# One shared set of four PSUM banks for the small matmuls of a hybrid decoder trunk, with small matmuls of one array tiling put together, the last-needed operand first, and the cumulative sum on the whole TensorE array

## The chip, the cores and the metric

The kernel runs on one core of one Trainium2 chip. The metric is the device time in microseconds (us) of one execution. The work is done by five engines that run side by side and wait for each other through semaphores: PE (TensorE, matrix multiplication), DVE (VectorE), ACT (ScalarE), POOL (GpSimd) and SP (SyncE, which issues most of the DMA transfers). Matmul results land in PSUM, which has eight banks of 128 partitions by 2 KB.

## The reference

Two layers on 256 tokens of width 1024. Each layer has three token mixers that are fed by one input projection, and then a feed-forward block.

```python
for l in range(DEPTH):                       # DEPTH = 2
    h = _rmsnorm(x, mix_norm[l])
    proj = (h @ w_in[l]).astype(jnp.float32)
    ret_c, fox_c, rwkv_c, gate_c = jnp.split(proj, splits, axis=-1)
    y_ret = _retention_branch(ret_c, ret_gn[l])          # q k^T * decay, then v; per head norm
    y_fox = _fox_branch(fox_c, ...)                      # softmax attention with a cumulated log forget gate
    y_rwkv = _rwkv7_branch(rwkv_c, ...)                  # recurrent state of 64x64 per head
    gates = jax.nn.sigmoid(gate_c).reshape(B, S, N_BRANCH, D)
    merged = (gates[:, :, 0] * (y_ret @ p_ret[l]) + gates[:, :, 1] * (y_fox @ p_fox[l])
              + gates[:, :, 2] * (y_rwkv @ p_rwkv[l]))
    x = x + merged @ w_out[l]
    h = _rmsnorm(x, ffn_norm[l])
    g, u = jnp.split(h @ w_gate_up[l], 2, axis=-1)
    x = x + (jax.nn.silu(g) * u) @ w_down[l]             # D_FF = 2816
```

Every mixer has four heads of 64 channels. All data are float32.

## The kernel before, in words

Large products. A float32 product is made of three matmuls with rounded operands (`mm3`, L304, L307, L308): high part by high part, low part of the data by high part of the weights, high by low. The weights come from HBM in pieces of 1 MB (tile `raw`, three buffers, issued by SP in the order in which they are used). ACT makes the high half `whi` of each (L287) and DVE the low half `wlo` (L288), 128x1024 at a time, four buffers each. On PE these products are rows named `mm`, `mv` and `mqk`, with 256 moving columns on the whole 128x128 array.

Small products. The mixers need many matmuls with 64 or 32 rows or columns. These run in a part of the array: the rows of the trace write the tiling as 64*128, 128*64, 64*64 or 32*32 (rows*columns of one part). Two heads of a pair lie in partitions 0 to 63 and 64 to 127, so their matmuls can use different parts.

- `rwkv`: the recurrence is cut into four chunks of 64 tokens (`NC` = 4, `C` = 64), 16 units for 2 head pairs `a`, 4 chunks `q` and 2 heads `h`. `pgm` (L807) are the masked products within a chunk, which DVE writes to `gg`; `ptr` (L842) are transposes. A triangular system is solved in steps: SP stores 16x16 blocks (`d`, L819), loads them rearranged (`lt`, L822), a loop on DVE inverts them (`ti`), SP stores (`d`, L872) and loads them again (`tb`, L877), DVE transposes (`dn`, L882, one instruction for each head `h`), and PE combines the blocks to 32 and 64 (`pn1` L887, `pn2` L894, `px1` L906, `px2` L914). Then `pu`, `par` (L935), `pU` (L947), the state from chunk to chunk `pS` (L957), and the output `py` (L972 within the chunk, L980 from the state).
- `fox`: the cumulative sum of the gates `pc` (L1061, L1062), scores `pl` (L1099) with the causal mask added by a matmul (L1101), transposes `px`, output `pyf` (L1123 to L1125).
- `ret`: scores `psc` (L1183, L1184), times the decay mask on DVE (`rsc`, L1185, L1186), output `pyr` (L1191 to L1193), head norm with `pnr` and `pvr`.

PSUM. Its eight banks are in three sets: four for the large products (tag `mm`), two for `rwkv` (tag `rw`), two for `fox`, `ret` and the norms (tag `fr`). A tile waits until the tile that had its bank before has been read.

What sets the order. `rwkv`, `fox`, `ret` and `gemms` (gate projections and merges) are generators. `mixers` takes turns among them: each `yield` gives a due time from the table `PACE`, and the generator that is due first goes on. The order of instructions on each engine comes from this program order and a scheduler that estimates when operands are ready. On the chip each engine works through its own list in that order. After the mixers a layer has the output projection, 22 pairs of gate and up columns, and the down projection, which are large products only.

Of the kernel before, what the change touches and what calls it, by code (L numbers as in the profile page):

```python
# [31 lines left out]
AHEAD = 3  # L32
PACE = {'hp_piece': 4.0, 'hp_gemm': 0.0, 'hp_rwkv': 0.0, 'hp_fox': 0.0, 'hp_ret': 0.0, 'hp_merge': 44.0, 'hp_turn': 0.0, 'gemms0': 3.04, 'gemms1': 3.31, 'gemms2': 5.65, 'gemms3': 3.34, 'gemms4': 32.96, 'gemms5': 10.98, 'rwkv0': 10.21, 'rwkv1': 11.2, 'rwkv2': 8.93, 'rwkv3': 1.29, 'rwkv4': 4.68, 'rwkv5': 0.99, 'rwkv6': 10.9, 'rwkv7': 6.78, 'rwkv8': 3.67, 'rwkv9': 15.39, 'rwkv10': 0.0, 'rwkv11': 0.1, 'rwkv12': 0.0, 'rwkv13': 4.53, 'rwkv14': 10.11, 'rwkv15': 3.46, 'rwkv16': 46.63, 'rwkv17': 6.78, 'rwkv18': 7.88, 'rwkv19': 1.76, 'fox0': 6.98, 'fox2': 4.26, 'fox3': 4.47, 'fox4': 9.38, 'ret0': 2.57, 'ret1': 2.4, 'ret2': 16.22, 'rwkv24': 0.61, 'rwkv22': 8.91, 'rwkv23': 25.79, 'rwkv20': 4.99, 'fox5': 10.77, 'ret4': 6.18, 'ret3': 0.0}
# [123 lines left out]
class Kernel:  # L157
    def __init__(self, ctx, tc, d, depth=DEPTH, debug=None):
# [15 lines left out]
        pz = self.ps.tile([P, T], F32, tag="fr", bufs=2, name="pz")  # L174
# [282 lines left out]
    def rstd(self):  # L457
# [6 lines left out]
        pn = self.ps.tile([P, 2], F32, tag="fr", bufs=2, name=self.nm("pn"))  # L464
# [24 lines left out]
    def gemm_n(self, width, xs, name="mv"):  # L489
        ps = [self.ps.tile([P, width], F32, tag="mm", name=self.nm(name)) for _ in range(2)]  # L490
# [48 lines left out]
    def mixers(self, l, xs):  # L539
# [87 lines left out]
    def ffn(self, l):  # L627
# [3 lines left out]
        with ExitStack() as st:  # L631
# [4 lines left out]
            for j in range(FT // 2):  # L636
                if j == 0:
                    pg = self.gemm_halves(xs, 7, tag="rw")
# [63 lines left out]
    def rwkv(self, l, rw):  # L702
# [3 lines left out]
        pt = lambda n: self.ps.tile([P, 2, T], F32, tag="rw", bufs=2, name=self.nm(n))  # L706
# [45 lines left out]
        pn = self.ps.tile([P, 2, 4], F32, tag="rw", bufs=2, name=self.nm("pnk"))  # L752
# [48 lines left out]
        for a in range(2):  # L801
            pg2 = [self.ps.tile([P, NC, 2 * C], F32, tag="rw", bufs=2, name=self.nm("pgm")) for _ in range(2)]
# [52 lines left out]
        pm = self.ps.tile([P, NP, 64], F32, tag="rw", bufs=2, name=self.nm("pm"))  # L855
# [35 lines left out]
        px = self.ps.tile([P, NP, C], F32, tag="rw", bufs=2, name=self.nm("pn2"))  # L891
# [29 lines left out]
        for a in range(2):  # L921
            pu = self.ps.tile([P, NC, 2 * C], F32, tag="rw", bufs=2, name=self.nm("pu"))
# [7 lines left out]
        for a in range(2):  # L930
            pa = self.ps.tile([P, NC - 1, 2 * C], F32, tag="rw", bufs=2, name=self.nm("par"))
# [10 lines left out]
        pu = self.ps.tile([P, 2, NC - 1, 64], F32, tag="rw", bufs=2, name=self.nm("pU"))  # L942
        for q in range(NC - 1):
            for a in range(2):
                for h in range(2):
                    u = unit(a, q, h)
                    nc.tensor.matmul(pu[hs[h], a, q, :], gg[:, u, 0:C], uw[:, u, :], start=q == a == 0, stop=q == NC - 2 and a == 1,  # L947
                                     tile_position=(0, h * 64))
        us = self.t2.tile([P, 2, NC - 1, 64], F32, tag="t2", name=self.nm("us"))
# [16 lines left out]
        py = [self.ps.tile([P, 2, 2, C], F32, tag="rw", bufs=2, name=self.nm("py")) for _ in range(2)]  # L966
        for q2 in range(NC // 2):
            for a in range(2):
                for h in range(2):
                    for e in range(2):  # L970
                        u = unit(a, 2 * q2 + e, h)
                        nc.tensor.matmul(py[h][hs[e], q2, a, :], gg[:, u, C:2 * C], uw[:, u, :], start=q2 == a == 0, stop=False,  # L972
                                         tile_position=(0, e * 64))
# [64 lines left out]
    def fox(self, l, fx):  # L1038
# [22 lines left out]
        nc.tensor.matmul(pc[0:8, :], lf[:, 0, :], c["tri"][:, 0, :], start=True, stop=False)  # L1061
        nc.tensor.matmul(pc[0:8, P:T], lf[:, 1, :], c["tri"][:, 1, P:T], start=False, stop=True)  # L1062
# [25 lines left out]
        for t in range(2):  # L1088
# [31 lines left out]
        for h in range(4):  # L1120
            a, s = h // 2, slice((h % 2) * 64, (h % 2) * 64 + 64)
            vs = slice(h * 64, h * 64 + 64)
            nc.tensor.matmul(py[s, a, 0:P], v[:, 0, vs], pT0[:, h, 0:P], start=True, stop=True)  # L1123
            nc.tensor.matmul(py[s, a, P:T], v[:, 0, vs], pT0[:, h, P:T], start=True, stop=False)
            nc.tensor.matmul(py[s, a, P:T], v[:, 1, vs], pT1[:, h, :], start=False, stop=True)  # L1125
# [116 lines left out]
```

## Time and profile before

| | |
|---|---|
| median of three runs | 795.45 us (795.17 to 798.04) |
| the profiled execution: its own time, its span | 795.98 us, 794.0 us |
| busy: PE, PEld (weight loads), DVE, ACT, POOL | 785.9, 761.8, 569.4, 403.6, 15.0 us |
| matmuls | 7010 |
| read from HBM, written | 136.97 MB, 1.33 MB |
| granted TensorE clock | 1.000 |

The span is the time from the first to the last instruction. Rows of the timeline give the start, the duration, the engine, the line of the kernel, the operation, the tile written and the tiles read, the tiling of the array (for PE) and the size; "x8" stands for eight instructions drawn as one row, and a bracket tells how long the engine had stood idle before the row and who released it. A float32 matmul of a small product shows as two records on PE (128 moving columns of `pgm`, one instruction, are two). Matmuls overlap on PE, so the distance between starts, not the duration, says what one costs. Layer 0's mixers lie at about 40 to 170 us, layer 1's at about 430 to 560 us.

### The profile page before, as it was taken

The page shows a single profiled execution, that of the slowest core. Times are in us where ns is not written, and L with a number is a line of the kernel's source. Part 1 is how long each engine was busy: PE and PEld are TensorE (multiplying, and loading weights), DVE is VectorE, ACT ScalarE, POOL GpSimd, SP SyncE. Part 2 cuts the span into 40 slices and gives each one's busy share as a digit, 9 for nine tenths or more (in the row PEclk, how much of TensorE's full clock was granted, in tenths as well). Part 3 has the DMA queues.
Part 4 walks back from the last instruction along what each step waited for, and adds up shares of the span by engine and source line. Part 5 has one row for each costly group of instructions (what it writes and reads, how often), then busy time and mean ns, then how long its engine had stood idle before and what let it go on. Part 6 is the DMA issues. An engine that isn't in the chain of part 4 may idle for free.

```text
span 794.0 us, 16539 instructions
## 1 busy us (share of the span) xinstructions
PE 785.9 (99%) x7010; PEld 761.8 (96%) x7010; DVE 569.4 (72%) x919; ACT 403.6 (51%) x563; POOL 15.0 (2%) x51
## 2 busy tenths in 40 slices
PE   8999999999999999999999999999999999999998
PEld 7999999999999999999998998998999999999998
DVE  5887888778866666656668798877787766666453
ACT  6577445345646544535446773544356544444331
POOL 3000000000000000000020000000000000000000
PEclk9999999999999999999999999999999999999999
DMA  8755434425555555555564453442355465564650
GB/s 319 259 173 181 152 118 167 133 74 220 192 193 201 178 206 193 171 195 199 199 203 174 174 173 111 167 166 81 134 213 211 161 213 176 196 210 162 208 192 27
DMA packets 28234, 140.42 MB, mean 177 GB/s; under 512 B 7648, under 2 KB 9216, under 8 KB 13184
## 3 DMA queue, kind: packets, MB, share of 16 engines
q1 hardware_dynamic: 28016, 139.10, 50.5%
q8 instruction: 55, 0.90, 0.5%
q10 hardware_dynamic: 144, 0.26, 0.1%
q14 instruction: 19, 0.16, 0.1%
HBM read 136.97 MB, written 1.33 MB: 174 GB/s over the span
## 4 chain that ended last, share of the span: by engine, by line
PE 94%; DVE 2%; DMA 2%; ACT 1%; issue 0%; SPq 0%; DVEq 0%; ACTq 0%
PE mm L304 27%; PE mm L307 27%; PE mm L308 27%; DVE wlo L288 1%; PE mqk L487 1%; PE mqk L486 1%; PE mqk L485 1%; DMA raw<-in_win 1%; ACT whi L287 1%; PE mv L485 1%; PE pgm L807 1%; PE mv L486 1%; PE mv L487 1%; DMA rsw<-rqk 1%; PE ptr L842 1%; PE psc L1183 0%
## 5 line engine op out<-in xcount | busy, mean ns | idle before, releaser
L287 ACT CAST whi<-raw 128x1024 fp32r<-128x1024 f32 (+1 forms) x257 | 264.9, 1033 | 311.4 <-PE mm L307 220.6
L288 DVE TENSOR_TENSOR wlo<-raw,whi 128x1024 fp32r<-128x1024 f32 (+1 forms) x257 | 308.7, 1203 | 152.0 <-ACT whi L287 151.4
L304 PE MATMUL mm<-xh,whi 128*128 128x256 f32 x1312 | 367.6, 280 | 1.6 <-ACT whi L287 1.3
L308 PE MATMUL mm<-xh,wlo 128*128 128x256 f32 x1264 | 351.0, 278 | 0.1
L307 PE MATMUL mm<-xl,whi 128*128 128x256 f32 x1264 | 350.6, 277 | 0.1
L304 PEld LDWEIGHTS mm<-xh,whi 128*128 128x128 f32 x1312 | 246.6, 188 | 4.0 <-ACT whi L287 1.5
L307 PEld LDWEIGHTS mm<-xl,whi 128*128 128x128 f32 x1264 | 237.5, 188 | 1.4 <-issue 0.5
L308 PEld LDWEIGHTS mm<-xh,wlo 128*128 128x128 f32 x1264 | 237.3, 188 | 1.1 <-issue 0.3
L307 PE MATMUL mm<-lo,whi 128*128 128x256 f32 x576 | 160.2, 278 | 0.2
L308 PE MATMUL mm<-hi,wlo 128*128 128x256 f32 x576 | 160.2, 278 | 0.0
L304 PE MATMUL mm<-hi,whi 128*128 128x256 f32 x576 | 160.0, 278 | 0.0
L307 PEld LDWEIGHTS mm<-lo,whi 128*128 128x128 f32 x576 | 108.2, 188 | 1.0 <-DVE lo L425 0.6
L304 PEld LDWEIGHTS mm<-hi,whi 128*128 128x128 f32 x576 | 108.2, 188 | 0.6 <-issue 0.3
L308 PEld LDWEIGHTS mm<-hi,wlo 128*128 128x128 f32 x576 | 108.1, 188 | 0.3
L650 DVE TENSOR_TENSOR h<-t,mm 128x512 f32<-128x512 f32 x22 | 15.1, 687 | 11.3 <-PE mm L308 8.4
L647 DVE TENSOR_TENSOR t<-mm,rstd 128x512 f32<-128x512 f32 (+1 forms) x24 | 15.1, 645 | 8.5 <-PE mm L308 8.5
L485 PE MATMUL mv<-whi,xh 128*128 128x260 f32 (+1 forms) x64 | 18.7, 293 | 0.0
L487 PE MATMUL mv<-whi,xl 128*128 128x260 f32 (+1 forms) x64 | 18.4, 287 | 0.0
L588 DVE TENSOR_TENSOR gate<-mm,rstd 128x512 f32<-128x512 f32 x24 | 16.4, 684 | 2.7 <-PE mm L308 2.7
L486 PE MATMUL mv<-wlo,xh 128*128 128x260 f32 (+1 forms) x64 | 18.4, 287 | 0.0
L597 DVE SCALAR_TENSOR_TENSOR gate<-gate,mm 128x512 f32<-128x512 f32 x24 | 15.9, 678 | 2.4 <-PE mm L308 2.3
L440 ACT ACTIVATE xh<-x,par 128x256 fp32r<-128x256 f32 x32 | 14.8, 501 | 2.5 <-DVE x L661 1.7
(257 smaller groups left out, 716.5 us busy)
## 6 DMA issues: line engine op xcount, KB each, us to landing
raw<-in_wg SPq DMA_DIRECT2D x44, 1024.0 KB
raw<-in_wgate SPq DMA_DIRECT2D x24, 1024.0 KB
raw<-in_wd SPq DMA_DIRECT2D x16, 1024.0 KB
raw<-in_win SPq DMA_DIRECT2D x13, 1024.0 KB
raw<-in_wo SPq DMA_DIRECT2D x8, 1024.0 KB
raw<-in_wd SPq DMA_DIRECT2D x8, 768.0 KB
raw<-in_wqk SPq DMA_DIRECT2D x4, 1024.0 KB
raw<-in_pp SPq DMA_DIRECT2D x4, 1024.0 KB
```

The costliest lines, as they stand in the source:

```text
L287: nc.scalar.copy(hi[:, :m * width], r)
L288: nc.vector.tensor_tensor(out=lo[:, :m * width], in0=r, in1=hi[:, :m * width].bitcast(F32), op=ALU.subtract)
L304: nc.tensor.matmul(out, wh, xh, start=first, stop=False)
L307: nc.tensor.matmul(out, wh, xl, start=False, stop=False)
L308: nc.tensor.matmul(out, wl, xh, start=False, stop=last)
L485: nc.tensor.matmul(out, xh[:, s], wh, start=first, stop=False)
L486: nc.tensor.matmul(out, xh[:, s], wl, start=False, stop=False)
L487: nc.tensor.matmul(out, xl[:, s], wh, start=False, stop=last)
L588: nc.vector.tensor_tensor(out=g, in0=ps, in1=self.b2(rstd), op=ALU.mult)
L597: nc.vector.scalar_tensor_tensor(out=g, in0=g, scalar=1.0, in1=ps, op0=ALU.add, op1=ALU.mult)
L647: nc.vector.tensor_tensor(out=t[:, o, :], in0=p, in1=self.bs(rstd, o), op=ALU.mult)
L650: nc.vector.tensor_tensor(out=h, in0=t, in1=pu, op=ALU.mult)
```

## The change

1. One set of PSUM banks. The tags `rw` and `fr` become one tag `sm` with `SM` = 4 banks; `mm` keeps 8 - `SM` = 4.
2. Groups of one tiling are joined. `psc`: the two heads of a pair, in alternation, and all four heads before one `yield` (before: a `yield` after each head). `pyf` and `pyr` go through the new `rows_out`, heads of a pair in alternation. `py`'s part from `uw` moves to directly behind `pU`, ahead of the state steps. The causal mask of `fox` is added once for two heads, ahead of the score matmuls.
3. The operand that is made last goes first: `h` in the order 1, 0 in `pn1`, `px1`, `px2`; `a` in the order 1, 0 in `par`; the second half of the chunks first in `py` (L980); `p1` first in `rows_out`.
4. The cumulative sum `pc` runs on the whole array: `lf`, 8 columns wide, is padded with zeros to 128 (two memsets on POOL more in all), and only the first 8 rows of the result are read, as before.

The large products, their order in a layer, the weights and the table `PACE` are as before. As the order falls out of generators and scheduler, it also moves in places that the diff doesn't name. Line numbers of the changed kernel are one higher than before up to L946 and drift after that.

On PE, in layer 0 around the outputs of `ret` and `fox` and the products `pgm`, the list before ends that stretch with the last third of `pyr` between transposes (`rsc` and `rv` are its operands, numbers are tile counters):

```order
L1192 MATMUL pyr_1315<-rsc_1150,rv_1054 64x128
L1193 MATMUL pyr_1315<-rsc_173_1151,rv_1054 64x128
L842 MATMUL ptr_1355<-con,rav_446 128x128 x4
L842 MATMUL ptr_1366<-con,rav_446 128x128 x2
L1191 MATMUL pyr_1315<-rsc_1150,rv_1054 64x128
L1192 MATMUL pyr_1315<-rsc_1150,rv_1054 64x128
L842 MATMUL ptr_1366<-con,rav_446 128x128 x2
L1193 MATMUL pyr_1315<-rsc_173_1151,rv_1054 64x128
L308 MATMUL mm_1377<-xh_145,wlo_1166 128x256
```

Now `pyr`, `pyf` and `pgm` stand in one stretch, and the transposes follow behind `pgm`:

```order
L308 MATMUL mm_1374<-xl_220,whi_1243 128x256
L1133 MATMUL pyr_1208<-rsc_173_1148,rv_1053 64x128 x2
L1133 MATMUL pyr_1208<-rsc_1147,rv_1053 64x128 x4
L1133 MATMUL pyr_1208<-rsc_173_1148,rv_1053 64x128 x2
L1133 MATMUL pyr_1208<-rsc_1147,rv_1053 64x128 x4
L1133 MATMUL pyf_1225<-pT_137_945,fv_668 64x128 x2
L1133 MATMUL pyf_1225<-pT_136_944,fv_668 64x128 x4
L1133 MATMUL pyf_1225<-pT_137_945,fv_668 64x128 x2
L1133 MATMUL pyf_1225<-pT_136_944,fv_668 64x128 x4
L808 MATMUL pgm_1272<-rav_446,bk_1005 128x128
```

What moved: `pyr`, which stood behind `pyf` and between `psc`, `pgm` and `ptr`, is whole and first, and `pyf` and `pgm` (sixteen matmuls, two tiles of a pair in alternation, the first one shown) come behind it without a large product between; `psc` stands ahead in a stretch of its own.

On PE, in the same layer, around `px1` (tile `px_269`; `t_263` is its operand from DVE for each head) the first instruction stood apart from the other fifteen, with large products (`mm`) between, before:

```order
L307 MATMUL mm_2057<-lo_1215,whi_1867 128x256
L906 MATMUL px_269_1899<-t_263_1860,gg 32x32
L308 MATMUL mm_2057<-hi_1214,wlo_1868 128x256
L304 MATMUL mm_2099<-hi_1214,whi_1938 128x256
L307 MATMUL mm_2099<-lo_1215,whi_1938 128x256
L906 MATMUL px_269_1899<-t_263_1860,gg 32x32 x15
```

Now the sixteen are one row:

```order
L308 MATMUL mm_2162<-xl_121,whi_1986 128x256
L309 MATMUL mm_2162<-xh_120,wlo_1987 128x256
L907 MATMUL px_269_1896<-t_263_1857,gg 32x32 x16
L305 MATMUL mm_2162<-xh_145,whi_1986 128x256
L308 MATMUL mm_2162<-xl_146,whi_1986 128x256
```

What moved: the first `px1` matmul went back to the others. `pn1` and `px2` changed likewise.

On DVE, in the same layer, the two transposes `dn` that `pn1` reads (the first for head 0, the second for head 1), and the other work between them, before:

```order
L588 TENSOR_TENSOR gate_1895<-mm_1814,rstd_432 128x512
L288 TENSOR_TENSOR wlo_1939<-raw_1865,whi_1938 128x1024
L597 SCALAR_TENSOR_TENSOR gate_1193<-gate_1193,mm_1937 128x512
L882 STREAM_TRANSPOSE dn_1792<-tb_1348 64x512
L597 SCALAR_TENSOR_TENSOR gate_1312<-gate_1312,mm_1955 128x512
L288 TENSOR_TENSOR wlo_1990<-raw_1987,whi_1989 128x1024
L882 STREAM_TRANSPOSE dn_1792<-tb_1348 64x512
```

and now:

```order
L598 SCALAR_TENSOR_TENSOR gate_1205<-gate_1205,mm_1934 128x512
L598 SCALAR_TENSOR_TENSOR gate_1326<-gate_1326,mm_1952 128x512
L289 TENSOR_TENSOR wlo_1987<-raw_1984,whi_1986 128x1024
L598 SCALAR_TENSOR_TENSOR gate_1433<-gate_1433,mm_1983 128x512
L883 STREAM_TRANSPOSE dn_1789<-tb_1345 64x512
L598 SCALAR_TENSOR_TENSOR gate_1515<-gate_1515,mm_2003 128x512
L289 TENSOR_TENSOR wlo_2037<-raw_1984,whi_2036 128x1024
L883 STREAM_TRANSPOSE dn_1789<-tb_1345 64x512
```

What moved: the first `dn` stands behind two more `gate` products and one more weight split (`wlo`); between the two `dn` stands the same as before. The first matmul of `pn1` now reads what the second `dn` writes.

On SP, the loads of weights (`raw`) and the two round trips of the triangular system, before:

```order
L819 DMA d_0_1332<-gg 16x8x16 x8
L822 DMA lt<-d_0_1332 64x256 x2
L277 DMA raw_1638<-in_wgate 128x2048
L277 DMA raw_1700<-in_pp 128x2048
L277 DMA raw_1865<-in_pp 128x2048
L277 DMA raw_1987<-in_wgate 128x2048
L872 DMA d_0_1333<-ti 64x128 x2
L277 DMA raw_2100<-in_wgate 128x2048
L877 DMA tb_1348<-d_0_1333 16x8x16 x8
```

and now:

```order
L820 DMA d_0_1329<-gg 16x8x16 x8
L278 DMA raw_1635<-in_wgate 128x2048
L823 DMA lt<-d_0_1329 64x256 x2
L278 DMA raw_1697<-in_pp 128x2048
L278 DMA raw_1862<-in_pp 128x2048
L278 DMA raw_1984<-in_wgate 128x2048
L278 DMA raw_2115<-in_wgate 128x2048
L873 DMA d_0_1330<-ti 64x128 x2
L878 DMA tb_1345<-d_0_1330 16x8x16 x8
```

What moved: one load of weights stands ahead of `lt`, and one more stands ahead of the store of `ti`; none is left between that store and the load of `tb`.

The core of the diff:

```diff
+SM = 4
...
-        ps = self.ps.tile([P, 2, T], F32, tag=tag, bufs=4 if tag == "mm" else 2, name=self.nm("mm"))
+        ps = self.ps.tile([P, 2, T], F32, tag=tag, bufs=8 - SM if tag == "mm" else SM, name=self.nm("mm"))
...
         px = self.ps.tile([P, NP, C], F32, tag="sm", bufs=SM, name=self.nm("pn1"))
         for p in range(NP):
-            for h in range(2):
+            for h in (1, 0):
                 nc.tensor.matmul(px[hs[h], p, :], nn[hs[h], p, :], dn[hs[h], p, :], ...)
...
         for p in range(NP):                                   # px1, and px2 alike
-            for h in range(2):
+            for h in (1, 0):
...
-        for a in range(2):
-            pa = self.ps.tile([P, NC - 1, 2 * C], F32, tag="rw", bufs=2, name=self.nm("par"))
+        for a in (1, 0):
+            pa = self.ps.tile([P, NC - 1, 2 * C], F32, tag="sm", bufs=SM, name=self.nm("par"))
...
+        py = [self.ps.tile([P, 2, 2, C], F32, tag="sm", bufs=SM, name=self.nm("py")) for _ in range(2)]
+        for q2 in range(NC // 2):                             # moved here from behind the pS steps
+            for a in range(2):
+                for h in range(2):
+                    for e in range(2):
+                        u = unit(a, 2 * q2 + e, h)
+                        nc.tensor.matmul(py[h][hs[e], q2, a, :], gg[:, u, C:2 * C], uw[:, u, :], ...)
         us = self.t2.tile([P, 2, NC - 1, 64], F32, tag="t2", name=self.nm("us"))
...
-        for q2 in range(NC // 2):
+        for q2 in (1, 0):
             for a in range(2):
-                for e in range(2):
+                for e in (1, 0):
                     for h in range(2):
...
-        na, lf = sm.tile([P, 2, 4], F32, name="na"), sm.tile([P, 2, 8], F32, name="lf")
+        na, lf = sm.tile([P, 2, 4], F32, name="na"), sm.tile([P, 2, P], F32, name="lf")
+        nc.gpsimd.memset(lf[:, :, 8:], 0.0)
...
-        nc.tensor.matmul(pc[0:8, :], lf[:, 0, :], c["tri"][:, 0, :], start=True, stop=False)
-        nc.tensor.matmul(pc[0:8, P:T], lf[:, 1, :], c["tri"][:, 1, P:T], start=False, stop=True)
+        nc.tensor.matmul(pc, lf[:, 0, :], c["tri"][:, 0, :], start=True, stop=False)
+        nc.tensor.matmul(pc[:, P:T], lf[:, 1, :], c["tri"][:, 1, P:T], start=False, stop=True)
...
+                nc.tensor.matmul(pl[:, :, t * P:n], self.identb, self.maskb.unsqueeze(1).broadcast_to([P, 2, P]), start=True, stop=False)
                 for i in range(2):
                     h = 2 * a + i
                     for b in range(t + 1):
-                        o = pl[:, i, b * P:(b + 1) * P]
-                        nc.tensor.matmul(o, qa[:, h, t * P:(t + 1) * P], ka[:, h, b * P:(b + 1) * P], start=True, stop=b < t)
-                        if b == t:
-                            nc.tensor.matmul(o, self.identb, self.maskb, start=False, stop=True)
+                        nc.tensor.matmul(pl[:, i, b * P:(b + 1) * P], qa[:, h, t * P:n], ka[:, h, b * P:(b + 1) * P],
+                                         start=False, stop=i == 1 and b == t)
...
+    def rows_out(self, py, v, p0, p1):
+        for a in (1, 0):
+            for first, t, q, p in ((True, 1, slice(P, T), p1), (False, 0, slice(P, T), p0), (True, 0, slice(0, P), p0)):
+                for i in (1, 0):
+                    h = 2 * a + i
+                    self.nc.tensor.matmul(py[i * 64:i * 64 + 64, a, q], v(t, h), p[:, h, :] if t else p[:, h, q], start=first,
+                                          stop=not first or q.start == 0)
...
-        for h in range(4):                                    # ret: one head, then a yield
+        for a in range(2):                                    # two heads in alternation, one yield behind all four
+            ps = [self.ps.tile([P, 384], F32, tag="sm", bufs=SM, name=self.nm("psc")) for _ in range(2)]
+            for t in range(2):
+                for i in range(2):
+                    s = slice(i * 64, i * 64 + 64)
+                    nc.tensor.matmul(ps[i][:, t * T:T + t * P], qk[s, 2 + a, t * P:(t + 1) * P], qk[s, a, t * P:], ...)
```

More of the change, by code (lines that the diff above doesn't have):

```diff
@@ L173, in __init__ @@
         nc.vector.memset(zero, 0.0)
-        pz = self.ps.tile([P, T], F32, tag="fr", bufs=2, name="pz")
+        pz = self.ps.tile([P, T], F32, tag="sm", bufs=SM, name="pz")
         for _ in range(22):
@@ L322, in gemm_halves @@
     def gemm_halves(self, xs, kcut=None, hook=None, tag="mm"):
-        ps = [self.ps.tile([P, T], F32, tag=tag, bufs=4 if tag == "mm" else 2, name=self.nm("mm")) for _ in range(2)]
+        ps = [self.ps.tile([P, T], F32, tag=tag, bufs=8 - SM if tag == "mm" else SM, name=self.nm("mm")) for _ in range(2)]
         n = len(xs) if kcut is None else KT
@@ L345, in first_pairs @@
     def first_pairs(self, xs):
-        ps = [self.ps.tile([P, 2, T], F32, tag=t, bufs=n, name=self.nm("mm")) for t, n in (("rw", 2), ("rw", 2), ("mm", 4), ("mm", 4))]
+        ps = [self.ps.tile([P, 2, T], F32, tag=t, bufs=n, name=self.nm("mm")) for t, n in (("sm", SM), ("sm", SM), ("mm", 8 - SM), ("mm", 8 - SM))]
         for kk in range(4):
@@ L366, in gemm_quad @@
     def gemm_quad(self, xs):
-        ps = [self.ps.tile([P, 2, T], F32, tag="mm", bufs=4, name=self.nm("mm")) for _ in range(2)]
+        ps = [self.ps.tile([P, 2, T], F32, tag="mm", bufs=8 - SM, name=self.nm("mm")) for _ in range(2)]
         for kk in range(KT // 2):
@@ L489, in gemm_n @@
     def gemm_n(self, width, xs, name="mv"):
-        ps = [self.ps.tile([P, width], F32, tag="mm", name=self.nm(name)) for _ in range(2)]
+        ps = [self.ps.tile([P, width], F32, tag="mm", bufs=8 - SM, name=self.nm(name)) for _ in range(2)]
         for k in range(KT):
@@ L637, in ffn @@
                 if j == 0:
[L638 removed]
+                    pg = self.gemm_halves(xs, 7, tag="sm")
                     _, dg = self.rstd()
@@ L751, in rwkv @@
         yield PACE["rwkv3"]
-        pn = self.ps.tile([P, 2, 4], F32, tag="rw", bufs=2, name=self.nm("pnk"))
+        pn = self.ps.tile([P, 2, 4], F32, tag="sm", bufs=SM, name=self.nm("pnk"))
         self.head_sums(sq, pn)
@@ L801, in rwkv @@
         for a in range(2):
-            pg2 = [self.ps.tile([P, NC, 2 * C], F32, tag="rw", bufs=2, name=self.nm("pgm")) for _ in range(2)]
+            pg2 = [self.ps.tile([P, NC, 2 * C], F32, tag="sm", bufs=SM, name=self.nm("pgm")) for _ in range(2)]
             for q in range(NC):
@@ L838, in rwkv @@
             for a in range(2):
-                ptr = self.ps.tile([P, 2 * NC, 64], F32, tag="rw", bufs=2, name=self.nm("ptr"))
+                ptr = self.ps.tile([P, 2 * NC, 64], F32, tag="sm", bufs=SM, name=self.nm("ptr"))
                 for q in range(NC):
@@ L890, in rwkv @@
         yield PACE["rwkv13"]
-        px = self.ps.tile([P, NP, C], F32, tag="rw", bufs=2, name=self.nm("pn2"))
+        px = self.ps.tile([P, NP, C], F32, tag="sm", bufs=SM, name=self.nm("pn2"))
         for p in range(NP):
@@ L910, in rwkv @@
         yield PACE["rwkv22"]
-        px = self.ps.tile([P, NP, B], F32, tag="rw", bufs=2, name=self.nm("px2"))
+        px = self.ps.tile([P, NP, B], F32, tag="sm", bufs=SM, name=self.nm("px2"))
         for p in range(NP):
-            for h in range(2):
+            for h in (1, 0):
                 nc.tensor.matmul(px[lo[h], p, :], v1[hi[h], p, :], tb[hi[h], p, h, B:], start=True, stop=True,
@@ L1198, in ret @@
         yield PACE["ret3"]
-        pn = self.ps.tile([P, 2, 4], F32, tag="fr", bufs=2, name=self.nm("pnr"))
+        pn = self.ps.tile([P, 2, 4], F32, tag="sm", bufs=SM, name=self.nm("pnr"))
         self.head_sums(sq, pn)
@@ L1202, in ret @@
         yield PACE["ret4"]
-        rs = self.ps.tile([P, 2, T], F32, tag="fr", bufs=2, name=self.nm("pvr"))
+        rs = self.ps.tile([P, 2, T], F32, tag="sm", bufs=SM, name=self.nm("pvr"))
         self.spread(yy, rs)
```

62 lines of the change are left out of this document (23 added, 39 removed).

## The prediction

> **What bounds the kernel now.** I read the page first (its busy times and the chain that ended last), then the groups of instructions by line, then the timeline of PE through the mixers of layer 0, and last the timelines of DVE and SP at the places where PE waits.
>
> ```profile
> PE 785.9 (99%) x7010; PEld 761.8 (96%) x7010; DVE 569.4 (72%) x919; ACT 403.6 (51%) x563; POOL 15.0 (2%) x51
> ...
> PE 94%; DVE 2%; DMA 2%; ACT 1%; issue 0%; SPq 0%; DVEq 0%; ACTq 0%
> ...
> L288 DVE TENSOR_TENSOR wlo<-raw,whi 128x1024 fp32r<-128x1024 f32 (+1 forms) x257 | 308.7, 1203 | 152.0 <-ACT whi L287 151.4
> ```
>
> PE is busy 99% of the span and carries 94% of the chain, so PE time that goes is time gained, unless PE then waits. DVE is busy 72% and does its work in pieces of up to 1.2 us (the weight split L288), which can stand ahead of a small operand that PE needs.
>
> But a busy PE need not be a PE at its pace. The next rows are one small group between large products, the second state step `pS`.
>
> ```profile
> 165.45 0.28 PE L308 MATMUL mm<-xh,wlo 128*128 128x256 f32 x1
> 165.65 0.33 PE L957 MATMUL pS<-S,ar 64*64 64x64 f32 x4
> 165.92 0.38 PE L304 MATMUL mm<-xh,whi 128*128 128x256 f32 x1
> 166.14 0.28 PE L307 MATMUL mm<-xl,whi 128*128 128x256 f32 x1
> 166.25 0.29 PE L308 MATMUL mm<-xh,wlo 128*128 128x256 f32 x1
> ```
>
> A large matmul is followed by the next after 0.11 us (166.14 to 166.25). From 165.45 to 166.14 pass 0.69 us, in which two large ones (0.23) and four small records ran: the small group cost 0.46. How little four records cost inside a group is seen below (`pn`: 0.33 us for 2 records, 1.14 for 30, so 0.029 each, 0.12 for four). The remaining 0.35 us is the price of leaving the 128*128 tiling and coming back. I call this an excursion. Half of it, 0.17, I take for a direct change between two small tilings. By the order, a layer has 22 excursions before and 13 now.
>
> **The change part by part, per layer.** First the outputs of `ret` and `fox` with `psc` and `pgm`.
>
> ```profile
> 91.06 0.28 PE L308 MATMUL mm<-xh,wlo 128*128 128x256 f32 x1
> 91.27 1.16 PE L807 MATMUL pgm<-rav,bk 64*128 64x128 f32 x8
> 92.35 0.39 PE L304 MATMUL mm<-xh,whi 128*128 128x256 f32 x1
> 92.57 0.28 PE L307 MATMUL mm<-xl,whi 128*128 128x256 f32 x1
> ...
> 95.94 1.16 PE L807 MATMUL pgm<-rav,bk 64*128 64x128 f32 x8
> ...
> 97.25 0.28 PE L304 MATMUL mm<-xh,whi 128*128 128x256 f32 x1
> 97.46 0.71 PE L1183 MATMUL psc<-rqk 64*128 64x256 f32 x4
> ...
> 98.54 0.28 PE L308 MATMUL mm<-xh,wlo 128*128 128x256 f32 x1
> ...
> 98.78 0.28 PE L307 MATMUL mm<-xl,whi 128*128 128x256 f32 x1
> ...
> 100.29 0.27 PE L1124 MATMUL pyf<-pT,fv 128*64 128x128 f32 x1
> 100.34 0.27 PE L1125 MATMUL pyf<-pT,fv 128*64 128x128 f32 x1
> ...
> 101.57 0.94 PE L807 MATMUL pgm<-rav,bk 64*128 64x128 f32 x14
> ...
> 107.05 0.29 PE L304 MATMUL mm<-xh,whi 128*128 128x256 f32 x1
> ```
>
> Before: `pgm` of one head alone, 91.06 to 92.57 less two large ones, is 1.28 us; it comes twice (91.27, 95.94), 2.57 in all. The first `psc` pair, 97.25 to 98.54, is 1.06. From 98.78 to 107.05, with `pyf`, the other `psc`, the other `pgm`, `pyr` and the transposes `ptr`, it is 8.04. Sum 11.7.
>
> Now: `psc` of all four heads is one excursion, 2 x 0.71 + 0.35 = 1.8. `pyr`, `pyf`, `pgm` and `ptr` follow each other with one excursion (0.35), one direct change (0.17), 24 + 24 output records at the step of 0.055 (100.29 to 100.34), 32 `pgm` records and eight transposes at the 0.11 of a whole-array matmul (0.9). For the `pgm` records two rows give the bounds: one head alone, 0.111 a record (eight take 1.16, the first 0.38 as in a group's start), and heads in alternation, 14 in 0.94, again 0.05 to 0.056. The order has them in alternation, so 32 x 0.055 = 1.8. With 2.6 for the outputs that is 5.8, and 7.6 in all. **Saved: 4.1.** If the records ran at 0.111, it would be 2.3.
>
> Next the triangular solve and the state.
>
> ```profile
> 145.84 0.33 PE L887 MATMUL pn<-dn,nn 64*64 64x64 f32 x2 [0.15 <-DVE dn L882]
> ...
> 148.45 1.14 PE L887 MATMUL pn<-dn,nn 64*64 64x64 f32 x30
> ...
> 153.71 0.21 PE L906 MATMUL px<-t,gg 32*32 32x32 f32 x2
> ...
> 154.41 0.69 PE L906 MATMUL px<-t,gg 32*32 32x32 f32 x30
> ...
> 160.48 0.87 PE L935 MATMUL par<-gg,wa 64*64 64x128 f32 x12 [0.20 <-ACT wa L927]
> ...
> 161.71 0.87 PE L935 MATMUL par<-gg,wa 64*64 64x128 f32 x12
> 162.51 0.92 PE L947 MATMUL pU<-uw,gg 128*64 128x64 f32 x24
> ...
> 168.31 0.69 PE L972 MATMUL py<-uw,gg 128*64 128x64 f32 x16
> ```
>
> `pn1`, `px1` and `px2` each had a first matmul of its own (rows x2, then x30): three excursions go, 1.05, and with the first the wait of 0.15. The two `par` groups, `pU`, four `pS` and `py` parts were six excursions with four direct changes; now `par`, `pU`, `py` from `uw` and the first `pS` stand together, then two `pS` and two `py` parts: five and two. That is 0.35 + 2 x 0.17 = 0.7; the wait of 0.20 for `wa` would go too. **Saved: 2.1.**
>
> The cumulative sum.
>
> ```profile
> 61.98 0.28 PE L308 MATMUL mm<-xh,wlo 128*128 128x256 f32 x1
> 62.19 0.60 PE L1061 MATMUL pc<-con,lf 128*8 128x256 f32 x2
> 62.62 0.38 PE L1062 MATMUL pc<-con,lf 128*8 128x128 f32 x2
> ...
> 63.16 0.28 PE L307 MATMUL mm<-xl,whi 128*128 128x256 f32 x1
> ...
> L1061 PEld LDWEIGHTS pc<-con,lf 128*8 128x8 f32 x4 | 0.2, 87 | 0.3
> ```
>
> 61.98 to 63.16 less two large ones is 0.95 us. On the whole array the four records keep their step (62.19 to 62.62, 0.215 each; half for the 128 columns), 0.65, and the excursion goes: **saved 0.3**. Bounds: nothing saved (the excursion is paid all the same) and 0.35. The memset that pads `lf` is on POOL, which is busy 2%; if it came late, `pc` would wait for one POOL instruction. The Trainium skill, "TensorE: Matmul & The Clock Gate", section "LDWEIGHTS (loading the stationary operand)", speaks against this part: a weight load takes a time that grows with its columns (P / 1.2 ns). By it the four loads of a layer grow from 8 to 128 columns, an estimate of 0.1 us each; were they in the open, `pc` would lose 0.1 us a layer where I count 0.3 gained, and the total would be 0.8 us higher. The row has 87 ns for 8 columns, where the rule would give 7, so the trace does not bear the small end of it out. I keep 0.3, since large matmuls, which load new weights of 128 columns each time, start every 0.11 us.
>
> The mask of `fox`: half of its eight small matmuls go and the rest are twice as wide; 4 x 0.055 = 0.2 at most, nothing at least; I take 0.2. The shared banks add no instruction; what they cost is a wait.
>
> Gross: 4.1 + 2.1 + 0.3 + 0.2 = 6.7 us a layer.
>
> **New waits.** Last-needed first means that a whole group starts only when its last operand is there.
>
> ```profile
> 147.52 0.71 DVE L882 STREAM_TRANSPOSE dn<-tb 64x512 f32<-64x512 f32 x1
> ```
>
> The first `pn1` matmul ran at 145.84; now it needs this second transpose, done at 148.23. If PE came as early as before, it would wait 2.4 us, and the large matmuls behind it in PE's list with it. By the order 78 large matmuls stood between `pm` and `pn1`, and 122 now, 5.0 us more cover, so nothing is the other bound; I take 0.5, nearer to the cover. Five more places have an operand just in time: `pyr` (the last `rsc`), the `pgm` group (a bank that another mixer's tile must leave), `pvr`, the joined `par` group (which waits for `wa` as before, 0.20), and `pv` (13 large matmuls less between `py` and it, and a weight split more on DVE). Each may lose from nothing to one 1.2 us split; I take 0.35 each. Sum 2.2, with 0.3 (the old waits alone) and 5 as its bounds. `par`, `pU`, `py` and `pS` in one row leave ACT's copy of `pU` hidden behind the `py` part; if `wa` is late, all four wait.
>
> Net 6.7 - 2.2 = 4.5 a layer, 9.0 for two. The large products keep their order, the feed-forward block has none of these groups. The profiled execution took 795.98 us (span 794.0, 2 us around it): 787.0 by its own time. It stands 0.5 above the median of the runs shown (795.45), so **786.4**.
>
> **The rivals.** What a run tells from no change is about 0.5%, 4 us: faster is below 791.5, slower above 799.4.
>
> No new waits: the 44 extra large matmuls cover what I charged. 13.4 us go: 782.0. For it speaks that PE waits for only 0.35 us a layer at these places now; against it, that DVE's list is as long as before.
>
> DVE becomes the bound around `psc` to `ptr`.
>
> ```profile
> 90.83:107.17 16.34, 16.31 (x146) 13.94 (x145) 14.12 (x24) 3.39 (x5) 0.00 (x0) 1.00 0.29 104
> ```
>
> In this stretch (columns: length, then PE, PEld, DVE, ACT, POOL busy) DVE works 14.12 of 16.34 us. If the same work had to fit, only 2.2 of the 4.1 could go, and PE would wait for one more split (1.2): 6.7 - 1.9 - 3.4 = 1.4 a layer, 792.6, no change to speak of. Against it: a good part of that DVE work is weight splits and gates that may lie elsewhere.
>
> Slower: the triangular solve comes late through SP.
>
> ```profile
> 133.75 0.33 SPq L277 DMA_DIRECT2D raw<-in_wgate  x1
> 134.13 1.13 SPq L872 DMA_DIRECT2D d<-ti  x2
> 137.86 0.34 SPq L277 DMA_DIRECT2D raw<-in_wgate  x1
> ...
> 144.60 0.35 SPq L277 DMA_DIRECT2D raw<-in_wgate  x1
> ```
>
> A weight load is issued only when a buffer is free, and SP's queue waits with it; loads follow each other by 4.1 and 6.7 us here. One more load now stands ahead of `lt` and one ahead of the store of `ti`. If both held the chain up by 6.7 us, it would be 13.4 late, 8.4 beyond the extra cover, with 1.7 of other waits 10.1 a layer: 795.45 + 2 x 3.4 = 802.2. It decides from 8.7 us of new waits a layer on. Against it: another load went from between the store and `tb`, and both must lie on a full buffer.
>
> That the change doesn't do what it says: joined records at 0.111 cost 1.8 a layer, 790.0, still faster.
>
> **How the numbers follow.** My forecast 0.69, no new waits 0.12, joined records slow 0.04, DVE the bound 0.12, late through SP 0.03. Faster by over 0.5%: 0.85; within: 0.12; slower: 0.03. The waits' bounds give 782.6 (0.3 a layer) to 792.0 (5); the range reaches down to the case without waits and up to the point of 0.5%: 781.5 to 791.5.
>
> **What would show it.** PE's busy sum falls by about 13 us and its matmul count by eight records for the mask alone; `pn`, `px` rows are x32; `pgm` starts lie 0.055 apart; `pc` shows 128*128. The waits of PE should name `dn`, `rsc`, `wa` and sum to 4 to 5 us more. I am wrong if PE waits more than 5 us a layer, most likely at `pn1` or `pyr`, or if the joined groups show more than 0.06 us a record.

## The result, and the profile after

The changed kernel takes 787.03 us (median of four runs, 786.09 to 787.42) against 796.54 for the kernel before in the same comparison (795.17 to 798.04): ratio 0.9878, 95% interval 0.9854 to 0.9903, faster by 1.2%. The forecast was 786.4. The profiled execution took 787.26 us with a span of 785.5, 8.7 and 8.5 less than before; the sum of the prediction had 9.0. The clock was 1.000.

From the page of the changed kernel, the busy times:

```profile
PE 774.2 (99%) x7002; PEld 754.9 (96%) x7002; DVE 569.7 (73%) x919; ACT 405.0 (52%) x563; POOL 17.8 (2%) x53
```

PE's busy time fell by 11.7 us, its matmuls by the eight of the mask. The span fell by less, so 3.2 us came back as idle time of PE. The list of what PE waited for (line, what it waited for: total, times, longest) names it; before, `dn` and `wa` stood in this list with 0.3 and 0.4, and `pv` not at all.

```profile
PE pn L888 <- DVE dn L883: 1.7, 2, 1.2
...
PE px L1116 <- DVE lg L1112: 0.9, 3, 0.3
PE pv L1000 <- DVE ysq L993: 0.8, 2, 0.4
PE par L936 <- ACT wa L928: 0.6, 2, 0.3
```

PE's timeline at the places that the prediction showed. First `psc` to `ptr`, now `psc` by itself and then one stretch, where there were six excursions:

```profile
96.75 1.58 PE L1192 MATMUL psc<-rqk 64*128 64x256 f32 x16
...
100.26 1.53 PE L1133 MATMUL pyr<-rsc,rv 128*64 128x128 f32 x24
101.62 1.48 PE L1133 MATMUL pyf<-pT,fv 128*64 128x128 f32 x24
103.03 2.64 PE L808 MATMUL pgm<-rav,bk 64*128 64x128 f32 x32
105.59 1.09 PE L843 MATMUL ptr<-con,rav 128*128 128x128 f32 x8
```

Then the triangular solve and the state. `pn1` and `px1` are one row each, `pn1` with a wait; `par`, `pU`, `py` and the first `pS` stand together, but the rest of `pS` and `py` is in four pieces.

```profile
147.76 1.15 PE L888 MATMUL pn<-dn,nn 64*64 64x64 f32 x32 [0.50 <-DVE dn L883]
...
153.77 0.69 PE L907 MATMUL px<-t,gg 32*32 32x32 f32 x32
...
160.40 1.53 PE L936 MATMUL par<-gg,wa 64*64 64x128 f32 x24 [0.31 <-ACT wa L928]
161.85 0.92 PE L948 MATMUL pU<-uw,gg 128*64 128x64 f32 x24
162.60 1.10 PE L957 MATMUL py<-uw,gg 128*64 128x64 f32 x32
163.64 0.45 PE L967 MATMUL pS<-us,ar 64*64 64x64 f32 x8
...
164.57 0.33 PE L967 MATMUL pS<-S,ar 64*64 64x64 f32 x4
...
165.38 0.33 PE L967 MATMUL pS<-S,ar 64*64 64x64 f32 x4
...
165.95 0.34 PE L982 MATMUL py<-S,ar 64*64 64x64 f32 x8
...
166.55 0.34 PE L982 MATMUL py<-S,ar 64*64 64x64 f32 x8
...
174.65 0.63 PE L1000 MATMUL pv<-con,ysq 128*128 128x128 f32 x4 [0.39 <-DVE ysq L993]
```

And the cumulative sum:

```profile
61.89 0.28 PE L309 MATMUL mm<-xh,wlo 128*128 128x256 f32 x1
62.01 0.59 PE L1064 MATMUL pc<-con,lf 128*128 128x256 f32 x2
62.44 0.38 PE L1065 MATMUL pc<-con,lf 128*128 128x128 f32 x2
...
62.78 0.28 PE L308 MATMUL mm<-xl,whi 128*128 128x256 f32 x1
```

From the starts of all matmuls I made a sum for each small tile, both layers together: the time from each start to the next, with what the large matmul at either end takes beyond its usual 0.1135 us. Waits are inside. These sums tell apart what the runs' times, which scatter by 1 to 3 us, do not. Each sum comes from one execution, and two rows move without an edit near them: `pv` reads 2.44 in e8, which changes only `pc`, and `pn1` depends on when the loads of `tb` land (see the rivals below). A few tenths in these two rows are not a finding. The kernel before took 796.54 us in the comparison of the change, 795.50 in that of e1 to e4, 795.31 in that of e5 to e8 and 796.50 in that of e9 and e10, so the ratios to it compare versions better than the medians do (the 795.45 of the tables is the median from before the change).

| us, both layers | before | changed | e1 banks only | e2 heads apart | e4 two sets |
|---|---|---|---|---|---|
| `pgm` | 7.42 | 5.13 | 4.69 | 4.69 | 9.11 |
| `psc` | 4.49 | 3.45 | 6.37 | 6.36 | 3.41 |
| `pyf` and `pyr` | 8.87 | 5.73 | 7.03 | 7.03 | 5.73 |
| `ptr` of `rav` | 2.58 | 1.87 | 1.88 | 1.88 | 1.91 |
| sum | 23.36 | 16.18 | 19.97 | 19.96 | 20.16 |
| time of the kernel, median | 795.45 | 787.03 | 792.79 | 789.96 | 788.51 |
| ratio to before | 1 | 0.9878 | 0.9966 | 0.9923 | 0.9904 |

| us, both layers | before | changed | e3 orders back | e5 `pn1` back | e6 `pn1`, `par` back | e7 `par` back | e9 `py` late | e10 `par` back, `py` late |
|---|---|---|---|---|---|---|---|---|
| `pn1` | 3.90 | 4.45 | 3.97 | 4.06 | 4.00 | 4.37 | 3.77 | 3.64 |
| `px1` and `px2` | 4.92 | 3.30 | 4.79 | 3.30 | 3.30 | 3.30 | 3.34 | 3.31 |
| `par` | 4.52 | 3.87 | 4.53 | 3.87 | 4.54 | 4.53 | 3.87 | 4.53 |
| `pU`, `py` from `uw` | 4.57 | 3.57 | 3.57 | 3.57 | 3.57 | 3.57 | 4.08 | 4.07 |
| `pS` | 3.02 | 2.63 | 2.15 | 2.61 | 2.14 | 2.14 | 2.82 | 2.81 |
| `py` from the state | 2.40 | 2.58 | 1.63 | 2.59 | 1.64 | 1.63 | 1.45 | 1.44 |
| `pv` | 0.91 | 2.05 | 0.90 | 2.44 | 0.91 | 0.91 | 2.74 | 2.45 |
| sum | 24.24 | 22.45 | 21.54 | 22.44 | 20.10 | 20.45 | 22.07 | 22.25 |
| time of the kernel, median | 795.45 | 787.03 | 786.21 | 787.56 | 784.99 | 783.93 | 787.83 | 786.91 |
| ratio to before | 1 | 0.9878 | 0.9880 | 0.9902 | 0.9866 | 0.9858 | 0.9884 | 0.9885 |

Outside these tables `pc` fell from 1.91 to 1.34 and the scores `pl` with their mask from 7.30 to 6.30; the transposes `px` of `fox` rose from 3.91 to 4.90.

### The profile page after: what moved, and what is told of

Its sections match the earlier page's. It is cut to its first block, busy times and chain, and to the rows that moved or that the text cites. A ratio compares the mean times of both kernels' runs of the same rounds, so it can differ in the third digit from the quotient of the medians.

```text
span 785.5 us, 16513 instructions
## 1 busy us (share of the span) xinstructions
PE 774.2 (99%) x7002; PEld 754.9 (96%) x7002; DVE 569.7 (73%) x919; ACT 405.0 (52%) x563; POOL 17.8 (2%) x53
## 4 chain that ended last, share of the span: by engine, by line
PE 91%; DVE 3%; DMA 2%; ACT 1%; SPq 1%; issue 1%; DVEq 0%; ACTq 0%
PE mm L309 26%; PE mm L305 26%; PE mm L308 26%; DVE wlo L289 1%; DMA d<-ti 1%; PE mqk L488 1%; PE mqk L487 1%; PE mqk L486 1%; DMA raw<-in_win 1%; ACT whi L288 1%; PE mv L488 1%; PE mv L486 1%; PE mv L487 1%; SPq L878 1%; PE pl L1103 1%
## 5 line engine op out<-in xcount | busy, mean ns | idle before, releaser
L590 ACT ACTIVATE gate<-gate 128x512 f32<-128x512 f32 x24 | 15.1, 629 | 5.6 <-DVE gate L589 5.6
```

What stands on the lines that cost most here:

```text
L590: nc.scalar.activation(g, g, AF.Tanh, scale=0.5)
```

## The experiments

The first question was which part carries the gain. My theory was that PE time is set by how often the array changes its tiling and whether two heads alternate, so by the order alone. The rival was that the rewritten loops do it and the banks only permit them.

### e1: the banks alone

```diff
-        tag="rw", bufs=2   /   tag="fr", bufs=2
+        tag="sm", bufs=SM                      # SM = 4; all else as in the kernel before
```

> The kernel before with the shared set of four banks and nothing else of the change. Theory 1 (bank sharing joins groups by itself, since a small group no longer waits for one of two banks of its mixer): the pgm matmuls of both pairs come out as one group with alternating heads, par and py as one group each, 16 excursions a layer against 22 and 13; 6 x 0.35 for excursions and 0.9 for pgm records make 3.0 a layer, 6 us of the 9: about 790 us. Theory 2 (the gain comes from the rewritten loops and orders, the banks only permit them): 795 to 797 us, pgm total on PE stays near 7.4 us.

792.79 us (792.11 to 795.30), ratio to before 0.9966 (0.9950 to 0.9982). PE's timeline of this run:

```profile
96.45 0.70 PE L1184 MATMUL psc<-rqk 64*128 64x256 f32 x2
...
97.30 1.12 PE L794 MATMUL pb<-rkk,con 128*128 128x512 f32 x2
98.35 0.70 PE L1184 MATMUL psc<-rqk 64*128 64x256 f32 x2
...
101.68 2.40 PE L808 MATMUL pgm<-rav,bk 64*128 64x128 f32 x31
```

`pgm` came out as one group and fell by 2.7 us, as the theory has it, with no loop rewritten. But with the old loops `psc` fell apart, one head at a time with `pb` between, and rose by 1.9, and `pn1` waits 1.8, as the transpose `dn` ahead of it stands idle for the loads of `tb`. A layer has 18 excursions, not the 16 expected. So the banks alone give about 3 us, half of what I expected: the order that they allow is better in one place and worse in another.

### e2: the heads of ret and fox apart

```diff
-        for a in range(2):                 # psc: two heads in alternation; pyf, pyr by rows_out
+        for h in range(4):                 # psc, pyf, pyr head by head, yield after each head of psc
```

> The changed kernel, but psc, pyf and pyr written head by head as before (a yield after each head of psc). Theory 1: pgm stays one group, so only psc in four pieces and two or three excursions a layer come back: 1.0 to 1.5 a layer, 789 to 790 us. Theory 2 (the joined loops of ret and fox carry the 3.6 a layer that this region lost): about 794 us.

789.96 us (788.35 to 790.61), ratio 0.9923 (0.9904 to 0.9943), as theory 1 expected, and `pgm` is the same 4.69 as in e1. The joined loops of `ret` and `fox` are worth 2.9 us in `psc` and 1.3 in the outputs, 0.4 of which `pgm` gives back. That is 3.8 for both layers, more than the 2 to 3 that theory 1 had, and it isn't excursions: from `psc` to `ptr` e2 has two a layer, as the changed kernel has, and one direct change more. What is lost is mostly the alternation of heads.

The time agrees only because something else got better. The order moved further down as well, and the tiles of the second table cost 19.9 here, against 22.45 with the change, although `par` keeps its new order. PE's timeline of e2, layer 1:

```profile
540.89 1.53 PE L936 MATMUL par<-gg,wa 64*64 64x128 f32 x24 [0.29 <-ACT wa L928]
...
550.13 0.45 PE L967 MATMUL pS<-S,ar 64*64 64x64 f32 x8
...
553.45 0.46 PE L982 MATMUL py<-S,ar 64*64 64x64 f32 x16
```

Both pairs' `pS` go together, `py` from the state is one group, and `pv` doesn't wait (its sum is 0.91).

### e4: the sets of banks as before

```diff
-        tag="sm", bufs=SM
+        tag="rw", bufs=2  (rwkv)  /  tag="fr", bufs=2  (the others)
...                                          # and py from uw behind the state steps again
```

> The changed kernel with the three sets of banks of before (4, 2, 2), and the part of py from uw back behind the state steps (two banks cannot hold it that early). Theory 1: pgm comes apart into four groups of one head pair, ptr and the rest as written; 4 excursions more and pgm records partly serial: 2 a layer, about 791 us. Theory 2: the loops are what counts, 787 to 788 us.

788.51 us (786.92 to 789.46), ratio 0.9904 (0.9886 to 0.9922). `pgm` in PE's timeline of this run:

```profile
90.77 1.16 PE L808 MATMUL pgm<-rav,bk 64*128 64x128 f32 x8
...
96.77 1.05 PE L808 MATMUL pgm<-rav,bk 64*128 64x128 f32 x8
...
98.94 1.05 PE L808 MATMUL pgm<-rav,bk 64*128 64x128 f32 x8
...
103.23 1.16 PE L808 MATMUL pgm<-rav,bk 64*128 64x128 f32 x8
```

With two banks for `rwkv`, `pgm` is four groups of eight records, one head each, 0.111 apart (before the change two of the heads alternated), and costs 9.11 us, 4.0 more than with shared banks: the mechanism of theory 1, and larger than I thought at this place. The time rose by only 1.5 by the medians and 2.1 by the ratios, since in this order the first table's loss meets other gains, with `par` in its new order here too: the `pv` wait is gone (0.91 against 2.05) and `py` from the state is one piece (1.45 against 2.58). Sharing and joining are thus both needed for low sums of `pgm` and `psc` at once; neither theory alone has it.

### e3, e5, e6, e7: the orders

```diff
-            for h in (1, 0):                   # pn1, px1, px2
+            for h in range(2):
...
-        for a in (1, 0):                       # par
+        for a in range(2):
```

e3 undoes all four, e5 only `pn1`, e6 `pn1` and `par`, e7 only `par`.

> The changed kernel, but pn1, px1, px2 and par in the orders of before (first-made operand first; py and rows_out stay). By my prediction four excursions a layer come back (1.4), the pn1 wait of 0.87 a layer falls to 0.15 or so and that of par changes little: net 0.5 to 0.8 a layer, 788 to 788.6 us. Rival: the lone first matmul costs less than the wait that it avoids, and the time falls to 786 us or below.

786.21 us (785.98 to 786.99), ratio 0.9880 against 0.9878 with the change: no difference that the times show, where I had expected a loss. In the second table `px1` and `px2` cost 0.37 more each a layer, almost the 0.35 of my excursion; what more than pays for it is in `pS`, `py` and `pv`. The next three runs took the orders apart.

> The changed kernel with only pn1 in its old order (head 0 first). Theory 1 (a lone first matmul costs one excursion, 0.37 us by the px rows of the runs so far, and the joined group waits 0.87 us a layer for the second dn): PE's share for pn1 falls from 4.45 to 3.9 us for both layers, the time by 0.5, to 786.5 us. Rival (the wait only moves, since the whole solve is late): pn1 falls, but px1 or par wait longer by the same, 787.0 us.

787.56 us (786.73 to 789.06), no gain, so theory 1 missed. The wait at `pn1` fell from 1.75 to 0.46, but the lone matmul's excursion ate most of that; the sum of the second table did not move (22.44 and 22.45). That the wait moved on, as the rival has it, is not shown: `px1` and `par`, which it named, are as with the change, and the 0.4 more at `pv` stands in e8 too. Nor is all of the 1.75 the order's doing, as 0.9 us of it is for a load of `tb` that landed late in that execution (see the rivals below). With the new order `pn1` reads from 3.64 (e10) to 4.45, with the old one 3.97 to 4.06 (e3, e5, e6), so what its order is worth stays open.

> The changed kernel with pn1 and par in their old orders, px1 and px2 in the new one. Theory 1 (it was par's new order, a = 1 first, that broke pS and py into single pieces and took the cover from pv; px1 and px2 gain 0.38 each a layer): pS falls by 0.5, py from S by 0.9, pv by 1.1, par rises by 0.7, pn1 falls by 0.5: 784.7 us, 1.5 below the run with all orders back. Rival (all four orders act alike, each a small loss): 786.2 us or more.

784.99 us (783.3 to 786.0), ratio to before 0.9866 (0.9846 to 0.9887), as theory 1 expected.

> The changed kernel with only par in its old order (a = 0 first). Theory 1: pS, py from S and pv as in the run with all orders back, pn1 still waits 0.87 a layer: 785.2 us. Rival (the gain of the run with all orders back came from pn1): 787 us.

783.93 us (783.2 to 785.79), ratio to before 0.9858 (0.9841 to 0.9875). PE's timeline of e7:

```profile
160.23 0.87 PE L936 MATMUL par<-gg,wa 64*64 64x128 f32 x12 [0.21 <-ACT wa L928]
...
161.46 0.87 PE L936 MATMUL par<-gg,wa 64*64 64x128 f32 x12
...
164.05 0.45 PE L967 MATMUL pS<-us,ar 64*64 64x64 f32 x8
...
164.97 0.45 PE L967 MATMUL pS<-S,ar 64*64 64x64 f32 x8
...
166.01 0.46 PE L982 MATMUL py<-S,ar 64*64 64x64 f32 x16
...
174.31 0.60 PE L1000 MATMUL pv<-con,ysq 128*128 128x128 f32 x4
```

`par` is split again (0.66 dearer), but `pS` of both pairs now goes together and `py` from the state is one group: 1.4 us less, and the wait of `pv` ends. e6 and e7 cannot be told apart by their times. The intervals of their ratios to before overlap with that of the change (0.9854 to 0.9903), so that the second table has to carry the reading: there the old order of `par` accounts for 2.0 us. These two are the fastest versions that the experiments gave. In the changed kernel, the step that lost was `par`'s new order. The order by itself is not the whole cause: e2 and e4 keep it, and their `pS` and `py` are in whole groups without a wait at `pv`. What in the rest of the order has to come with it was not tested.

### e8: the cumulative sum on 8 columns

```diff
-        nc.tensor.matmul(pc, lf[:, 0, :], c["tri"][:, 0, :], start=True, stop=False)      # lf padded to 128
+        nc.tensor.matmul(pc[0:8, :], lf[:, 0, :], c["tri"][:, 0, :], start=True, stop=False)
```

> The changed kernel with the cumulative sum on 8 columns of the array again, and without the memset. By my prediction 0.3 a layer comes back: pc takes 1.9 us on PE for both layers instead of 1.34, the time 787.6 us. By the rival from the column count of the weight load, pc's loads of 128 columns cost more than the excursion: pc would take about 1.2 us for both layers, the time 786.8 us.

787.78 us (787.60 to 788.19), ratio 0.9904 (0.9889 to 0.9918); `pc` takes 1.91 us again. The time alone could not show 0.6 us, and `pv` reads 0.4 more here as well; the sum of `pc` carries the reading. The weight loads, from this run and from the changed kernel (least, median and largest ns):

```profile
L1063 PEld LDWEIGHTS pc<-con,lf x4: 85/86/88, 62.2 to 448.2; 128*8 128x8 f32 x4
```

```profile
L1064 PEld LDWEIGHTS pc<-con,lf x4: 187/189/190, 61.9 to 448.1; 128*128 128x128 f32 x4
```

The load did become 0.1 us longer, as the Trainium skill ("TensorE: Matmul & The Clock Gate", section "LDWEIGHTS (loading the stationary operand)") has it for 120 more columns, but it does not show in the matmuls' starts: two records of `pc` take 0.43 us (62.01 to 62.44), as they do on 8 columns in the kernel before (62.19 to 62.62), and the excursion is gone.

### e9 and e10: the part of py from uw late again

```diff
-        py = [...]; matmuls from uw        # directly behind pU
...
+        py = [...]; matmuls from uw        # behind the state steps
```

> The changed kernel with the part of py from uw back behind the state steps (par keeps its new order). Theory 1 (what counts is how many pieces pS and py come in, and how many large matmuls stay between py and pv): pU and py from uw cost 0.9 more for both layers, py from S 0.9 less, and 65 large matmuls instead of 59 before pv end the pv wait (1.1 less): 786 us. Rival (my prediction: moving that part saves an excursion and two direct changes, 0.7 a layer): 788.4 us.

787.83 us (785.73 to 788.22), a miss. The terms on PE went as expected in sign (`pU` and `py` from `uw` 0.5 more instead of 0.9, `py` from the state 1.1 less instead of 0.9), but `pv` waits more (1.48 us), though 65 large matmuls stand ahead of it instead of 59. DVE's timeline of the changed kernel at that place, and of e7, shows what stands ahead of `pv`:

```profile
172.62 0.42 DVE L993 TENSOR_TENSOR ysq<-py,y 128x256 f32<-128x256 f32 x1
172.96 1.22 DVE L289 TENSOR_TENSOR wlo<-raw,whi 128x1024 fp32r<-128x1024 f32 x1
174.09 0.42 DVE L993 TENSOR_TENSOR ysq<-py,y 128x256 f32<-128x256 f32 x1
```

```profile
172.08 0.76 DVE L993 TENSOR_TENSOR ysq<-py,y 128x256 f32<-128x256 f32 x2
172.80 1.23 DVE L289 TENSOR_TENSOR wlo<-raw,whi 128x1024 fp32r<-128x1024 f32 x1
```

In the changed kernel the second half of `ysq`, which `pv` needs, stands behind one more weight split of 1.2 us; in e7 both halves come ahead of it. In e9 the chain to `ysq` starts late. On ACT the squares of the two halves of `py` have a cast of 1.06 us and a gate of 0.62 between them, and on DVE a split stands ahead of `yss`, the first step there:

```profile
168.59 0.39 ACT L988 ACTIVATE ysq<-py 128x256 f32<-128x256 f32 x1 [4.58 <-PE py L982]
...
170.58 0.36 ACT L988 ACTIVATE ysq<-py 128x256 f32<-128x256 f32 x1
...
170.18 1.23 DVE L289 TENSOR_TENSOR wlo<-raw,whi 128x1024 fp32r<-128x1024 f32 x1 [0.33 <-ACT whi L288]
171.32 0.68 DVE L990 TENSOR_REDUCE yss<-ysq 128x8 f32<-128x512 f32 x1
```

From the start of the last group of `py` on PE (168.16 and 166.30) to `yss` pass 3.2 us here and 1.1 in e7; most of the difference is ACT's. From `yss` to the end of `ysq` both take 5.4. So the number of large matmuls alone does not decide: e9 with 65 waits and e7 with 66 doesn't. What the scheduler puts ahead of the chain on ACT and DVE decides with it.

> The run with only par in its old order, and in addition the part of py from uw back behind the state steps. Theory 1: pU +0.6, py from uw +0.3, py from S -0.2, pS +0.9 for both layers, and with 59 large matmuls before pv its wait of 1.1 is back: 786.4 us, 2.5 above that run. Rival (the move is worth nothing once par is in its old order): 784 us.

786.91 us (785.86 to 789.28), near the 786.4 of theory 1, against 783.93 for e7. Early `py` is worth 1.8 us in the second table (2.5 without `pn1`) and 2.1 by the ratios, once `par` is in its old order; the medians' 3.0 come from two comparisons in which the kernel before differs by 1.2. With `par`'s new order, late `py` costs nothing in the table (22.07 against 22.45).

## Why the prediction was right, step by step

The forecast is 0.6 us off, and a part of that closeness is luck. PE's busy time fell by 11.7 us where about 13 were forecast, and its idle time rose by 3.2 where its waits were to rise by 4 to 5: too much saving and too much waiting cancelled.

- The count of excursions, 22 and 13 a layer, is what the two traces show. The price of one, 0.35 us: the two `px` groups, split in e3 and whole in the change, give 0.37 each. Right.
- `psc` to `ptr`, 4.1 a layer: (23.36 - 16.18) / 2 = 3.6. Mis-sized at `pgm`: 32 records took 2.56 us (103.03 to 105.59), not 1.8. Pairs of heads do start 0.112 apart, but each half of the group begins slowly (its second pair comes 0.21 after the first) and the second waits for its bank, which the prediction had among the waits. By the prediction's own sign of being wrong, more than 0.06 us a record, the step fails at `pgm` (0.080) and holds at `pyr` and `pyf` (0.057 and 0.059).
- Solve and state, 2.1 a layer: without `pv`, (23.33 - 20.40) / 2 = 1.5. Of the waits of 0.35 a layer that were to go, none went: `pn1` and `par` wait 1.2 a layer now. Without any waits the tiles fell from 22.6 to 18.0, 2.3 a layer. The sum was near, but for a wrong reason in part: three excursions went at `pn1`, `px1`, `px2`, while `par` in one piece saved one and `pS` and `py`, which came apart, cost two. I took the number of pieces from the order and did not ask which edit made them; e7 is the answer for this kernel, with the limit that e2 and e4 set to it.
- `pc`, 0.3 a layer: 0.29. The mask, 0.2: 0.5 for all of `pl`. A part that I had not counted: before, the score record behind a mask matmul took 0.165 us to the next start, and now 0.11 like the others.
- New waits, 2.2 a layer. With the 0.35 of old waits that I let go, the prediction has waits rise by 1.85. Measured rises: the waits of `pn1` and `par` 0.83, the sums of `pv` 0.57, of `px` in `fox` 0.5 and of `pvr` 0.2, together 2.1. Not all of these sums is waiting, since PE's whole idle time rose by 1.6 a layer. The total held roughly, the places less so: I charged `pyr`, which waits for nothing, and had not thought of the transposes of `fox`, which wait for `lg` (0.9 us).
- The rivals. DVE did not become the bound: from `psc` to `ptr` PE waits 0.15 us a layer, 0.10 of it at `pgm` for DVE to read `pyf`. SP brought no late solve in layer 0: by DVE's timeline the second `dn` starts, without idle time before it, as the weight split ahead of it ends, so the wait of `pn1` there is for the split and not for a transfer. In layer 1 a late transfer does hold it up: the second `dn` stands idle 0.89 us for a load of `tb`, and `pn1` waits 1.25, the longest of the waits listed above. SP issued the eight loads of `tb` in 5.18 us there and in 3.65 in layer 0; in e3, e5 and e6 it took 3.65 in layer 1 too, and `dn` did not wait. So this rival came true in one layer, on a scale of 1 us and not of 13. What lengthened the issue is not shown. The rows are DVE's in layer 0, DVE's and PE's in layer 1, and SP's in both:

```profile
145.76 1.20 DVE L289 TENSOR_TENSOR wlo<-raw,whi 128x1024 fp32r<-128x1024 f32 x1
147.00 0.71 DVE L883 STREAM_TRANSPOSE dn<-tb 64x512 f32<-64x512 f32 x1
...
533.84 0.71 DVE L883 STREAM_TRANSPOSE dn<-tb 64x512 f32<-64x512 f32 x1 [0.89 <-DMA tb<-d]
...
534.61 1.15 PE L888 MATMUL pn<-dn,nn 64*64 64x64 f32 x32 [1.25 <-DVE dn L883]
...
141.27 3.65 SPq L878 DMA_DIRECT2D tb<-d  x8
...
527.29 5.18 SPq L878 DMA_DIRECT2D tb<-d  x8
```

## What to carry to other kernels

Count the changes of array tiling in the order and price one from the trace (0.35 to 0.37 us here); on a PE that is 99% busy this came within a microsecond of a change of one per cent, with errors of over one in the saving and in the waits that cancelled. The count is not all: e2 has 12 excursions a layer, one fewer than the changed kernel, and is slower, as the heads of `psc` do not alternate. Put the operand that is made last first only where its group then still has cover: in the changed kernel the same edit saved 0.4 us a group at `px` and cost 2 us at `par`, where the steps behind it came apart. That they did because they needed the other half first is my reading and not shown; in e2 and e4 the same order did no such harm. So test such an edit by itself, in the order in which it will run. When several mixers share banks, rewrite their loops along with it, since each of the two alone left almost 4 us of the gain in the region concerned (first table).

## What the runs showed of the hardware that was not expected

One head's `pgm` records start 0.111 us apart, wherever they stand (e4, four groups); two heads in alternation start as pairs, 0.112 from pair to pair, so 0.056 a record. On the whole array `pc` begins without any price (61.89 to 62.01 is an ordinary step) and costs 0.66 us in all (61.89 to 62.78 less two large ones), against 0.95 on eight columns, although each of its weight loads is twice as long.
